# A one-core encoder kernel: order of the MLP's first weight casts, buffers of the pair sums, and place of the last block's left half

## The chip, the cores and the metric

The kernel runs on one core of one Trainium2 chip. The metric is the device time of one execution in microseconds (us), the median of several timed runs. A core has a matrix engine (TensorE, PE in the profile; its weight loads are PEld), a vector engine (VectorE, DVE), an activation engine (ScalarE, ACT), a general engine (GpSimd, POOL) and a queue engine (SyncE, SP) that issues nearly all of the DMA transfers here. Each engine works through its own list of instructions in order and waits at an instruction until its inputs and its output buffer are ready.

## What is computed

One layer of an encoder on two inputs with shared weights: a prompt of 512 rows and a sample of 1024 rows, width 1024. The core of the reference:

```python
def _trunk(x, ...):
    h = _rmsnorm(x, norm_attn_g)
    z = h @ w_in                       # q, k, v and two conv inputs
    a_out = _window_attn(q, k, v, bias, band, attn_sink)
    c = ca * sigmoid(cb)
    c = silu(_layernorm(_dwconv(c, conv_dw_w, conv_dw_b)))   # 31 taps
    x = x + concatenate([a_out, c]) @ w_out
    h = _rmsnorm(x, norm_ffn_g)
    u = _dwconv(h @ w_up, ffn_dw_w, ffn_dw_b)                # 3 taps
    x = x + (silu(u[..., :D_FF]) * u[..., D_FF:]) @ w_down   # D_FF = 2816
    return _rmsnorm(x, norm_final_g)
```

All data are float32. The kernel keeps their precision by splitting each operand into a high part, rounded to the matrix engine's format, and a low part, the rest (`split`, line 227: ACT casts, POOL or DVE subtracts), and by multiplying high by high, high by low and low by high: three matmuls where one would do for rounded numbers.

## The kernel before

**Buffers.** All working tiles come from a host-side list of slots (`Slots`, line 74): 15 of class `q` (4096 bytes in each partition), 4 of class `c` (4224), 61 of class `h` (2048), 2 of class `d` and 32 small ones. A tile takes the smallest free slot that it fits, the one that has been free for longest first, and an argument `among` restricts it to a class. The next user of a slot has to wait for the last reader of the tile that was there.

**Order.** The program is written in one order, and a planner orders each engine's instructions by it and by a simulated time line; an instruction that is written later can be moved ahead when the earlier ones are not ready in that simulation. `tc.issue_after(ins)` binds the instructions written under it to come after `ins` on the engine of `ins`. From line 1381 on the matrix engine's order is the written one (`manual_schedule`); the other engines are still planned. Beside the main stream there is a queue of generators, `side`: after every few matmuls `tick` (line 320) moves it on by as many steps (`yield`) as `pace` says.

**Stages and lines that matter here.**

- Up to about 332 us: the first norm, the combined projection `w_in`, attention and convolution of the prompt. At the end of the prompt's chain, `make_h2` (line 883) scales the prompt's four row blocks, and `transposed` (line 296) turns them on PE in 8 chunks (L301) and evicts each chunk as a high part by ACT (L303) and a low part by DVE (L304). It appends the two eviction instructions of each chunk to the list `marks`, so the last 8 entries are those of the prompt's MLP input. Meanwhile the sample's depthwise convolution of 31 taps goes on: most taps on DVE (L402), five to seven for each piece as a product on ACT (L394) that POOL adds up (L395); DVE adds POOL's sum at the end (L410).
- The prompt's MLP, `for k in range(NJ)` (line 1067), 22 steps from about 332 to 648 us. Each step takes a pair of 1024x128 weight tiles (gate and value half) that were loaded (`want_up_raw`, L224) and split (`want_up`, line 944, by `split`: the cast is L230, the low part L231), and multiplies them with the turned blocks in `up_mm`. The very first half uses the order of L343: for each chunk the high and then the low weights with the high input, and after these the low input with the high weights; all others go by L347, L348 and L350. The first pair is split at lines 1041 and 1042, with no order given. During the MLP, `side` runs `sample` (line 1045): the sample's attention (scores L672), then the loads of `w_out` for its output projection, column half 0 at line 1055 and half 1 at 1064, eight loads there in one go.
- `gate` (line 990) stores each step's result to DRAM (`gt`). For pairs 7 to 10 it calls `pair_sums` (line 1011) directly; for pairs 0 to 6 `pair_sums` runs later from `side` and loads both parts back into a tile of class `c` (L1014). Four POOL steps (L1021 to L1027) write four combinations into a tile `r`, which is stored to DRAM (`gb`, L1028). `r` needs 4096 bytes and so takes a `q` slot, of which the split weights and the loaded ones are also made.
- The sample's output projection by row blocks of 128 (`out_half`, line 828: 24 matmuls for a column half, L838 to L840, then the sum of squares on ACT, L849, and the scale on POOL, L214 and L215), from about 605 to 740 us. `scaled` (line 1101) then multiplies the block by its scale and the norm's weights; for the last four blocks (`t == 1`) it does the right half and the left half (L1110), and forms the sums `s1` (L1085), `s2` and a difference (L1088) with the block's partner, the inputs of a Strassen-like scheme of seven products.
- From about 733 us on, the first products of the sample's up projection run; from about 746 us the last five of seven input combinations are turned in four chunks each (two are turned before) (`turned`, line 1131: transposes L1135, ACT's high part L1137, DVE's low part by `sub`, L1088), between those products (`prod`, L1212 to L1214). These five come in the order 4, 6, 7, 5, 3. Combination 4 needs the right halves alone, 6 needs `s2`. Four PSUM banks take the transposes in turn (`turn_bank`). The products go on to about 1180 us; the down projection follows from about 1165 (L1556 to L1558) and the final norm.

Of the kernel before, what the change touches and what calls it, by code (L numbers as in the profile page):

```python
# [173 lines left out]
def tile_hybrid_encoder(ctx: ExitStack, tc: tile.TileContext, xs, xsT, rel_bias, norm_attn_g, w_in,  # L174
# [16 lines left out]
    sb = Slots(lambda tag: homes[tag[0]], dict(q=(15, 4096), c=(4, 4224), h=(61, 2048), d=(2, 2176), s=(32, 64)), "q", KEEP)  # L191
# [35 lines left out]
    def split(raw, dve=False):  # L227
        shape = list(raw.t.shape[1:])
        hi, lo = sb.tile(shape, F32R), sb.tile(shape, F32R)
        nc.scalar.copy(hi[:], raw[:])  # L230
        ins = (nc.vector if dve else nc.gpsimd).tensor_tensor(lo[:], raw[:], hi[:].bitcast(F32), op=ALU.subtract)  # L231
        if not dve:
            ended["pool"] = ins.ins
        return hi, lo
# [59 lines left out]
    marks = []  # L294
# [39 lines left out]
    def drain(queue):  # L334
        while queue:
            advance(queue)
# [291 lines left out]
    NB = len(blocks)  # L628
# [16 lines left out]
    def sink_columns():  # L645
        for h in range(0, NH, 2):
            t = sb.tile([2, NT])
            for n in range(2):
                nc.vector.tensor_copy(t[:, n, 0:1], nsink[:, h + n:h + n + 1])
            score_rows.append(t)  # L650
# [116 lines left out]
    def attention(u0, u1, then={}):  # L767
        yield from scores(u0)
        for u in range(u0, u1):
            if u + 1 < u1:  # L770
                yield from scores(u + 1)
            yield from values(u)
            if u in then:
                yield from then[u]

    def load_cat(i):
        rawcat[i] = sb.tile([NT])
        nc.sync.dma_start(rawcat[i][:], catd[blocks[i][1]])
# [10 lines left out]
    def conv_norm(i):  # L789
        G, b = blocks[i]  # L790
        if G["g"] == 0:
            drain(convs)
        cat = cat_of(i, 1)
        if i not in cvs:
            load_conv(i)
            yield 0.0
        cv = cvs.pop(i)
        if G["g"] == 1:
            split_cat(i, nc.vector)
        pt = bank("norm")  # L800
        for c in range(4):
            nc.tensor.transpose(pt[:, c * P:(c + 1) * P], cv[:, c, :], ident[:])
        st, mv, rs = sm(6), sm(2), sm(1)
        nc.vector.bn_stats(st[:], pt[:])
        nc.vector.bn_aggr(mv[:], st[:])
        rstd_of(mv[:, 1:2], 1.0, rs[:])
        xh = sb.tile([CCH])
        nc.vector.tensor_scalar(xh[:], pt[:], mv[:, 0:1], rs[:], op0=ALU.subtract, op1=ALU.mult)
        del pt
        for _ in range(YN if G["g"] == 0 else 3):  # L810
            yield 0.0
        p2 = bank("norm")
        for c in range(4):
            nc.tensor.transpose(p2[:, c * P:(c + 1) * P], xh[:, c * P:(c + 1) * P], ident[:])
        y, t = sb.tile([4, P]), sb.tile([4, P])
        for c in range(4):
            nc.scalar.activation(y[:, c, :], p2[:, c * P:(c + 1) * P], AF.Identity,
                                 scale=lng[:, c:c + 1], bias=lnb[:, c:c + 1])
        nc.scalar.activation(t[:], y[:], AF.Tanh)
        nc.vector.scalar_tensor_tensor(t[:], t[:], 1.0, y[:], op0=ALU.add, op1=ALU.mult)  # L820
        nc.scalar.copy(cat[0][:], t[:])
        nc.vector.tensor_tensor(cat[1][:], t[:], cat[0][:].bitcast(F32), op=ALU.subtract)
        yield 0.0
# [33 lines left out]
    def load_wo(kc, n):  # L857
        raw = wor[kc, n] = sb.tile([NT])
        s = slice(n * NT, (n + 1) * NT)
        if kc < 4:  # L860
            for kv in range(NKV):
                r0 = (kv * GRP + kc) * HD
                nc.sync.dma_start(raw[kv * HD:(kv + 1) * HD, :], w_out[0, r0:r0 + HD, s])
        else:
            nc.sync.dma_start(raw[:], w_out[0, kc * P:(kc + 1) * P, s])

    def split_wo(kc, n, dve=False):
        wo[kc, n] = split(wor.pop((kc, n)), dve)
# [52 lines left out]
    def want_up_raw(k, half):  # L921
        if k < len(seq):
            upr[k, half] = chunk_raw(w_up[0], half * FF + seq[k][1] * P)
# [20 lines left out]
    def want_up(k, half):  # L944
        if k < len(seq):
            upw[k, half] = split(upr.pop((k, half)))
# [37 lines left out]
    HT = NT // 2  # L984
# [26 lines left out]
    def pair_sums(p, e=None, o=None):  # L1011
        if e is None:
            g = sb.tile([2, NT], among="c")
            nc.sync.dma_start(g[:], gt[p][:])  # L1014
            yield 0.0
            yield 0.0
            e, o = g[:, 0, :], g[:, 1, :]
        r = sb.tile([4, HT])
        gp = nc.gpsimd.tensor_tensor
        with tc.issue_after(ended["pool"]):  # L1020
            gp(r[:, 0, :], e[:, HR], o[:, HR], op=ALU.add)  # L1021
        yield 0.0
        gp(r[:, 1, :], e[:, HL], e[:, HR], op=ALU.subtract)
        yield 0.0
        gp(r[:, 2, :], r[:, 0, :], e[:, HL], op=ALU.subtract)
        yield 0.0
        gp(r[:, 3, :], o[:, HL], r[:, 2, :], op=ALU.subtract)  # L1027
        nc.sync.dma_start(gb[p][:], r[:])  # L1028
        yield 0.0
# [8 lines left out]
        gate(k, ug[0], uv[0])  # L1038

    use.update(attn="ab", gate="b")  # L1040
    for half in range(2):
        want_up(0, half)
    want_up_raw(1, 0)
    load_bias()
    def sample():
        sink_columns()
        yield from attention(8, 24)
        kt.clear(), vt.clear(), qt.clear(), bias.clear(), score_rows.clear()
        use.update(norm="a")
        pace.update(rate=RN)  # L1050
        for m in range(KC + WOA):
            if m in (2, 4):
                load_cat(m // 2 + 3)
            if m < KC:
                load_wo(m, 0)
            if m >= WOA:
                split_wo(m - WOA, 0, True)
                yield 0.0
        drain(late)
        for m in range(NE):  # L1060
            yield from conv_norm(4 + m)
        load_conv(4 + NE)
        for kc in range(KC):
            load_wo(kc, 1)

    pace.update(rate=RD, late=CD)
    for k in range(NJ):
# [14 lines left out]
    L, R = slice(0, NT), slice(NT, W2)  # L1082

    def add(out, a, b, eng=None):
        (eng or nc.vector).tensor_tensor(out, a, b, op=ALU.add)  # L1085

    def sub(out, a, b, eng=None):
        (eng or nc.vector).tensor_tensor(out, a, b, op=ALU.subtract)  # L1088
# [8 lines left out]
    gFb = sb.tile([D])  # L1097
    nc.sync.dma_start(gFb[:], norm_ffn_g[0].partition_broadcast(P))
    A, rows = {}, {}

    def scaled(i):

        t, b = divmod(i - 4, 4)
        x = rows[t, b] = sb.tile([D])
        if t == 0:
            nc.vector.scalar_tensor_tensor(x[:], x1[i][:], rs2[:, i:i + 1], gFb[:], op0=ALU.mult, op1=ALU.mult)
            x1.pop(i)
            return
        for s in (R, L):
            nc.vector.scalar_tensor_tensor(x[:, s], x1[i][:, s], rs2[:, i:i + 1], gFb[:, s], op0=ALU.mult, op1=ALU.mult)  # L1110
        x1.pop(i)
        e = rows[0, b]
        s1 = rows["s1", b] = sb.tile([NT])
        s2 = rows["s2", b] = sb.tile([NT])
        add(s1[:], x[:, L], x[:, R])
        sub(s2[:], s1[:], e[:, L])
        sub(x[:, L], e[:, L], x[:, L])
        if i >= NB - 2:
            last_sum(b)
# [11 lines left out]
    def turned(i, get):  # L1131
        for c in range(4):
            held, ap = get()
            for b in range(4):
                nc.tensor.transpose(ap[:, b * P:(b + 1) * P], block_rows(i, b)[:, c * P:(c + 1) * P], ident[:])  # L1135
            hi, lo = A[i, c] = (sb.tile([NT], F32R), sb.tile([NT], F32R))
            nc.scalar.copy(hi[:], ap)  # L1137
            sub(lo[:], ap, hi[:].bitcast(F32))
            held = None
            yield 0.0  # L1140
        key = {6: "s2", 5: "s1", 7: 1, 3: 0}.get(i)
        for b in range(4):
            rows.pop((key, b), None)
# [122 lines left out]
    drain(side)  # L1266
    wo.clear()
    cats.clear()
    gFb = None
    for guard in reversed(ps_guards):  # L1270
        guard.__exit__(None, None, None)
    ps2 = [ctx.enter_context(tc.tile_pool(name=f"pw{i}", bufs=1, space=bass.MemoryType.PSUM)) for i in range(2)]
# [25 lines left out]
    def second(j, between=None):  # L1298
        prod(st[j]["x"][:, L], j, 2, False, True, between)
# [88 lines left out]
    def chain(*gens):  # L1388
        for g in gens:
            yield from g  # L1390

    def every(n, gen):

        for c in range(4):
            for _ in range((n * (c + 1)) // 4 - (n * c) // 4):
                next(gen, None)
            yield

    turns = chain(*(turned(i, turn_bank) for i in (4, 6, 7, 5, 3)))
    firsts = []  # L1400
    for j in range(2):
        st[j] = dict(x=wide())
# [4 lines left out]
    second(0, every(7, turns))  # L1407
    fourth(0, every(7, turns), True)
    second(1, chain(every(8, turns)))
    for _ in turns:  # L1410
        raise RuntimeError("turns left")
    pt_guard.__exit__(None, None, None)
# [410 lines left out]
```

## Time and profile before

| what | us |
|---|---|
| median of 3 timed runs | 1498.74 |
| lowest and highest | 1498.42, 1499.70 |
| the profiled execution | 1496.34 |
| its span, first to last instruction | 1494.6 |

The profiled execution is one of its own, with 1.74 us around its span; its granted TensorE clock was 0.996 of the full one on average. In the rows of groups and of the time-ordered view, a line says start, duration, engine, kernel line, operation, tiles (out <- in), shape and count; what stands in brackets is the engine's idle time before, and what ended it. A row of the stretches has the stretch, its length, PE's busy time with the number of matmuls, the granted clock, the DMA engines' share and GB/s. A row of the waits has who waited for whom, the sum, the number and the longest. Successive matmuls overlap: each has a duration of about 0.39 us but the next one starts 0.23 us later.

### The profile page before, as it was taken

Reading aid. Unit: us, or ns where it says so; the run is one execution under the profiler, and the core shown is the slowest. Engines: PE = TensorE matmul, PEld = TensorE weight load, DVE = VectorE, ACT = ScalarE, POOL = GpSimd, SP = SyncE. Lnnn points to the kernel's source line nnn. Section 1 sums busy time; section 2 is a strip of 40 time slices with the busy share of each in tenths; the row PEclk is TensorE's granted clock in tenths of the full one; section 3 lists DMA queues with packets and bytes.
Section 4 is the critical chain, followed back from the end, with each engine's and each line's share of the span. In section 5 each row is a group of like instructions: output and inputs, shape, how many; then the busy total and the mean of one; then the engine's idle time right before and its main releaser. Section 6 shows DMA issues by size and latency. Waiting matters only on the chain.

```text
span 1494.6 us, 19858 instructions
## 1 busy us (share of the span) xinstructions
PE 1474.5 (99%) x6808; PEld 1220.8 (82%) x6808; DVE 1138.6 (76%) x1616; ACT 797.9 (53%) x1417; POOL 682.0 (46%) x540
## 2 busy tenths in 40 slices
PE   9989999999999999999999999999999999999998
PEld 7878888887888888788878888888887888888886
DVE  4999998678689976666768777777776845568884
ACT  7635665335777776543455455544444633434354
POOL 7842444235756566654425555555544000003345
PEclk9999999999999999999999999999999999999999
DMA  8863347275434446783313333333332672356644
GB/s 279 280 199 80 100 120 196 85 221 153 144 112 132 127 133 206 225 287 115 113 57 106 106 106 106 102 99 103 103 109 81 226 264 85 109 173 227 210 173 169
DMA packets 221761, 225.08 MB, mean 151 GB/s; under 512 B 12331, under 2 KB 161843, under 8 KB 221532
## 3 DMA queue, kind: packets, MB, share of 16 engines
q1 hardware_dynamic: 221660, 223.82, 46.7%
q8 instruction: 53, 0.87, 0.2%
q14 instruction: 48, 0.39, 0.1%
HBM read 164.77 MB, written 60.05 MB: 150 GB/s over the span
## 4 chain that ended last, share of the span: by engine, by line
PE 47%; DVE 2%; ACT 1%; issue 0%; DMA 0%; POOL 0%; POOLq 0%; DVEq 0%; ACTq 0%
PE w L1212 9%; PE w L1213 9%; PE w L1214 9%; PE w L1556 7%; PE w L1558 7%; PE w L1557 7%; DVE q L1088 0%; DMA q<-in_w_up 0%; PE t L1135 0%; ACT q L1198 0%; DVE q L1343 0%; DVE q L1342 0%; DVE q L1110 0%; DVE h L1088 0%; ACT h L1137 0%
## 5 line engine op out<-in xcount | busy, mean ns | idle before, releaser
L231 POOL TENSOR_TENSOR q<-q,q 128x1024 fp32r<-128x1024 f32 x71 | 172.7, 2438 | 117.4 <-ACT q L230 42.1
L1088 POOL TENSOR_TENSOR q<-q,q 128x512 fp32r<-128x512 f32 x101 | 142.0, 1413 | 157.4 <-ACT q L1198 145.2
L1088 DVE TENSOR_TENSOR h<-h,h 128x512 fp32r<-128x512 f32 (+2 forms) x202 | 157.3, 811 | 63.0 <-ACT h L1092 26.3
L1558 PE MATMUL w<-h,h 128*128 128x512 f32 x462 | 179.7, 389 | 0.0
L1556 PE MATMUL w<-h,h 128*128 128x512 f32 x458 | 178.2, 389 | 0.0
L1557 PE MATMUL w<-h,h 128*128 128x512 f32 x458 | 178.2, 389 | 0.0
L1212 PE MATMUL w<-h,q 128*128 128x512 f32 x448 | 175.0, 391 | 2.0 <-ACT w L1296 1.4
L1214 PE MATMUL w<-h,q 128*128 128x512 f32 x448 | 174.3, 389 | 0.0
L1213 PE MATMUL w<-h,q 128*128 128x512 f32 x426 | 165.8, 389 | 0.0
L347 PE MATMUL u<-h,q 128*128 128x512 f32 x368 | 146.6, 399 | 0.6 <-ACT q L230 0.6
L348 PE MATMUL u<-h,q 128*128 128x512 f32 x368 | 144.1, 391 | 0.0
L350 PE MATMUL u<-h,q 128*128 128x512 f32 x360 | 141.4, 393 | 0.1
L402 DVE SCALAR_TENSOR_TENSOR c<-c,cvw,c 128x512 f32<-128x512 f32 x184 | 137.8, 749 | 2.6
L1085 POOL TENSOR_TENSOR q<-q,q 128x1024 f32<-128x1024 f32 x12 | 32.5, 2717 | 229.0 <-DMA h<-gb 190.0
L1092 ACT CAST h<-h 128x512 fp32r<-128x512 f32 x120 | 71.9, 620 | 98.2 <-DVE h L1088 41.2
L347 PE MATMUL b<-h,q 128*128 128x512 f32 x264 | 106.1, 402 | 3.9 <-ACT q L230 3.9
L348 PE MATMUL b<-h,q 128*128 128x512 f32 x264 | 104.7, 397 | 0.0
L350 PE MATMUL b<-h,q 128*128 128x512 f32 x264 | 104.3, 396 | 0.0
L1558 PEld LDWEIGHTS w<-h,h 128*128 128x128 f32 x462 | 86.7, 188 | 18.2
L1212 PEld LDWEIGHTS w<-h,q 128*128 128x128 f32 x448 | 84.1, 188 | 20.6 <-ACT w L1296 1.8
L1557 PEld LDWEIGHTS w<-h,h 128*128 128x128 f32 x458 | 86.0, 188 | 17.9
L1556 PEld LDWEIGHTS w<-h,h 128*128 128x128 f32 x458 | 86.0, 188 | 17.7
(447 smaller groups left out, 3641.6 us busy)
## 6 DMA issues: line engine op xcount, KB each, us to landing
q<-in_w_up SPq DMA_DIRECT2D x88, 512.0 KB, 4.1
ga<-q SPq DMA_DIRECT2D x64, 256.0 KB, 2.0
h<-ga SPq DMA_DIRECT2D x57, 256.0 KB, 3.4
q<-in_w_in SPq DMA_DIRECT2D x28, 512.0 KB, 4.9
h<-in_w_down SPq DMA_DIRECT2D x52, 256.0 KB, 3.6
q<-in_x_sample SPq DMA_DIRECT2D x15, 512.0 KB, 7.5
x1d<-q SPq DMA_DIRECT2D x11, 512.0 KB, 2.9
gt<-h SPq DMA_DIRECT2D x22, 256.0 KB, 3.1
```

Source lines behind the costliest of these rows:

```text
L231: ins = (nc.vector if dve else nc.gpsimd).tensor_tensor(lo[:], raw[:], hi[:].bitcast(F32), op=ALU.subtract)
L347: nc.tensor.matmul(out, whi[:, kc, :], hi[:], start=(kc == 0), stop=False)
L348: nc.tensor.matmul(out, whi[:, kc, :], lo[:], start=False, stop=False)
L350: nc.tensor.matmul(out, wlo[:, kc, :], hi[:], start=False, stop=(kc == KC - 1))
L402: nc.vector.scalar_tensor_tensor(acc[:], src(t), w(t), acc[:], op0=ALU.mult, op1=ALU.add)
L1088: (eng or nc.vector).tensor_tensor(out, a, b, op=ALU.subtract)
L1212: nc.tensor.matmul(out, whi[:, s], hi[:], start=(start and c == 0), stop=False, **go)
L1213: nc.tensor.matmul(out, whi[:, s], lo[:], start=False, stop=False, **go)
L1214: nc.tensor.matmul(out, wlo[:, s], hi[:], start=False, stop=(stop and c == 3), **go)
L1556: nc.tensor.matmul(out, sh[:, c], th[:], start=(p == 0), stop=False)
L1557: nc.tensor.matmul(out, sh[:, c], tl[:], start=False, stop=False)
L1558: nc.tensor.matmul(out, sl[:, c], th[:], start=False, stop=(p == NPAIR - 1))
```

## The change

Three groups of edits:

1. The two splits of the MLP's first weight pair are written under `tc.issue_after`: the cast of the first half comes behind ACT's eviction of chunk 2 of the prompt's turned blocks (`marks[-6]`), the cast of the second half behind that of chunk 7 (`marks[-1]`).
2. In `pair_sums` the result tile `r` is taken from class `c` in place of `q`, in the direct calls (pairs 7 to 10) and the later ones (0 to 6). The eight `w_out` loads of column half 1 in `sample` get a `yield` each.
3. For the last row block, `scaled` does the right half alone and keeps the rest for later. `opening` wraps the turning of combination 4: after the second of its four chunks is written it does the left half, `s1`, `s2`, the difference and the last sum (`left_sums`). The tile of the norm's weights, `gFb`, and the block's `x1` are held until then.

```diff
@@ pair_sums
-        r = sb.tile([4, HT])
+        r = sb.tile([4, HT], among="c")
@@ before the prompt's MLP
-    for half in range(2):
-        want_up(0, half)
+    for half, mark in enumerate(marks[-6::5]):
+        with tc.issue_after(mark[0]):
+            want_up(0, half)
@@ sample
         for kc in range(KC):
             load_wo(kc, 1)
+            yield 0.0
@@ scaled
-        for s in (R, L):
+        def part(s):
             nc.vector.scalar_tensor_tensor(x[:, s], x1[i][:, s], rs2[:, i:i + 1], gFb[:, s], op0=ALU.mult, op1=ALU.mult)
+
+        part(R)
+        if i == NB - 1:
+            held.append((i, part))
+        else:
+            left_sums(i, part)
+
+    held = []
+
+    def left_sums(i, part):
+        b = (i - 4) % 4
+        x = rows[1, b]
+        part(L)
         x1.pop(i)
         e = rows[0, b]
         s1 = rows["s1", b] = sb.tile([NT])
...
@@ after the output projection
-    gFb = None
...
@@ the turned combinations
-    turns = chain(*(turned(i, turn_bank) for i in (4, 6, 7, 5, 3)))
+    def opening():
+        for n, _ in enumerate(turned(4, turn_bank)):
+            if n == 1:
+                left_sums(*held.pop())
+            yield
+
+    turns = chain(opening(), *(turned(i, turn_bank) for i in (6, 7, 5, 3)))
...
     second(1, chain(every(8, turns)))
+    gFb = None
```

## The prediction

> **What bounds the kernel now.** I read the page's busy table first, then the busy time in stretches, then the list of what TensorE (PE) waited for, and last the time-ordered view around each wait that the change touches.
>
> ```profile
> span 1494.6 us, 19858 instructions
> PE 1474.5 (99%) x6808; PEld 1220.8 (82%) x6808; DVE 1138.6 (76%) x1616; ACT 797.9 (53%) x1417; POOL 682.0 (46%) x540
> 332.00:342.00 10.00, 7.81 (x46) 1.00 0.94 295
> 740.00:768.00 28.00, 26.13 (x151) 1.00 0.22 69
> 768.00:1120.00 352.00, 351.72 (x1552) 1.00 0.32 103
> ```
>
> PE is busy for 1474.5 of 1494.6 us at a granted clock of 1.00 in these stretches (the column behind the count). In the long stretch from 768 to 1120 us it misses 0.28 us. The number of matmuls doesn't change, so all that the change can win lies in the 20.1 us in which PE is idle: 2.19 of them between 332 and 342, 1.87 between 740 and 768. VectorE (DVE), ScalarE (ACT) and GpSimd (POOL) have spare time; they matter only where PE waits for them:
>
> ```profile
> PE b L347 <- ACT q L230: 3.9, 1, 3.9
> PE a L672 <- DVE h L304: 2.2, 2, 2.0
> PE w L1212 <- ACT w L1296: 1.4, 1, 1.4
> PE t L1135 <- DVE h L1088: 1.3, 1, 1.3
> PE u L347 <- ACT q L230: 0.6, 1, 0.6
> ```
>
> Three of these five belong to the change: L672 behind L304 (the start of the prompt's MLP, where the first weight casts are), the 0.6 at L347 (a weight cast of the later MLP), and L1135 (the turned blocks of the sample). The 3.9 (first projection) and the 1.4 at L1296 (late in the sample's up projection) stand at code that isn't edited. So the ceiling is 2.2 + 0.6 + 1.3 = 4.1 us, and 0.2% of 1498.74, about what a measurement of this kernel tells from no change, is 3.0 us.
>
> **Part 1, the first weight casts.** ACT, DVE, POOL and PE in the stretch of that wait:
>
> ```profile
> 321.67 0.19 ACT L849 ACTIVATION_READ_ACCUMULATOR h<-q 128x1 f32 x1
> 325.35 1.05 ACT L230 CAST q<-q 128x1024 fp32r<-128x1024 f32 x1 [3.49 <-DMA q<-in_w_up]
> 326.31 3.78 ACT L394 ACTIVATE h<-c,cvw 128x512 f32<-128x512 f32 x6
> 330.00 1.82 ACT L303 ACTIVATE h<-a,vecs 128x512 fp32r<-128x512 f32 x3
> 338.42 0.68 ACT L303 ACTIVATE h<-a,vecs 128x512 fp32r<-128x512 f32 x1
> 326.48 2.41 POOL L231 TENSOR_TENSOR q<-q,q 128x1024 fp32r<-128x1024 f32 x1 [3.72 <-PE b L350]
> 330.17 8.11 POOL L395 TENSOR_TENSOR h<-h,h 128x512 f32<-128x512 f32 x6 [1.28 <-ACT h L394]
> 338.31 0.69 DVE L410 TENSOR_TENSOR h<-c,h 128x512 f32<-128x512 f32 x1 [2.23 <-POOL h L395]
> 338.92 1.40 DVE L304 SCALAR_TENSOR_TENSOR h<-a,vecs,h 128x512 fp32r<-128x512 f32 x2
> 328.09 0.49 PE L301 MATMUL a<-ident,q 128*128 128x128 f32 x3
> 332.10 1.07 PE L343 MATMUL u<-h,q 128*128 128x512 f32 x4
> 333.02 0.60 PE L301 MATMUL a<-ident,q 128*128 128x128 f32 x4
> 333.37 0.71 PE L343 MATMUL u<-h,q 128*128 128x512 f32 x2
> 339.71 0.50 PE L672 MATMUL a<-q,h 128*128 128x256 f32 x2 [2.03 <-DVE h L304]
> ```
>
> Read it backwards. PE stood for 2.03 us before L672, for DVE's L304; two of these stood behind L410, which waited for POOL's six conv additions; POOL had begun them only when ACT's six conv products were done (330.17, the products ended at 326.31 + 3.78 = 330.09); and these stood behind the weight cast, which sat on ACT for 3.49 us waiting for its weights to land. The edit puts the cast behind the turned activation of chunk 2, the last of the group of three that ends at 331.82. ACT is then free at 321.86: products to about 325.7, POOL's additions from there to 325.7 + 8.11 = 333.8, or 336.2 when the 2.41 us of the cast's low part goes between them. L410 comes 2.1 us or more earlier than 338.31, and the 2.2 us of idle time go.
>
> What is late next is the weight itself. The turned blocks' last transposes of chunks 0 to 2 end at 328.58, so L303 x3 runs from 328.6 to 330.4, the cast (1.05) to 331.5, and the low part (2.41 on POOL, behind at most one addition of 1.35) ends between 333.9 and 335.3, against 328.89 now. PE wants the high part at 332.10, which holds, and the low part one matmul later, since the first product alternates high and low weights. Twelve transposes (four take 0.35, from 333.02 to the next matmul at 333.37) are other work for 1.05 us; after the first product (0.23) and these, PE would stand from 332.10 + 1.28 = 333.4 to between 333.9 and 335.3: a new wait of 0.5 to 1.9 us, of which I take the smaller half, 0.9. **Part 1: -2.2 + 0.9 = -1.3**, between -2.2 and a loss that I price under the rivals. The second cast, moved behind the last turned activation, costs nothing that PE sees: it can't hold that activation up (338.42 now), and while it and its low part are made, PE has the rest of the 24 products with the first weights, at 0.227 us each (352 / 1552, from the long stretch).
>
> **Part 2, the pair sums' buffers and the spread loads.** Rows around the later cast, and the stores of pair sums:
>
> ```profile
> 607.23 1.05 ACT L230 CAST q<-q 128x1024 fp32r<-128x1024 f32 x1 [3.88 <-DMA gb<-q]
> 608.33 0.50 PE L347 MATMUL u<-h,q 128*128 128x512 f32 x1 [0.59 <-ACT q L230]
> DMA to landing us min/median/max: 2.6/4.2/7.2
> 635.55 0.74 POOL L1021 TENSOR_TENSOR q<-c 128x256 f32<-128x256 f32 x1 [1.72 <-DMA gb<-q]
> ```
>
> The cast's q buffer was a pair sum's result, so the cast waited 3.88 us for that sum's store (the third row: the stores of L1028). With the result in a c buffer the cast can start about 3.8 us sooner and PE's 0.59 us go: **-0.6**. The price is on the four c buffers, which now hold two tiles for each loaded pair: a pair must wait until an earlier store has landed. One such wait is there already (1.72 us, on POOL). More of them, 2.6 to 7.2 us each, fall on POOL, which is idle for half of the span; the work behind them there is the small variance steps for normalised blocks, and one block's output product of 24 matmuls at 0.227, 5.4 us, covers a median store. I count 0, from -0.3 to +1.8 (7.2 less 5.4). The eight `w_out` loads are issued at the same cost on SP, only further apart; what they feed is the output products after the MLP, so 0.
>
> **Part 3, the last block's left half.**
>
> ```profile
> 745.63 0.75 DVE L1110 SCALAR_TENSOR_TENSOR q<-c,rs,q 128x512 f32<-128x512 f32 x1 [1.53 <-POOL rs L215]
> 746.30 1.78 DVE L1110 SCALAR_TENSOR_TENSOR q<-c,rs,q 128x512 f32<-128x512 f32 x1
> 746.24 1.29 POOL L1088 TENSOR_TENSOR q<-h,q 128x512 fp32r<-128x512 f32 x1 [0.65 <-ACT q L1198]
> 748.11 0.69 DVE L1085 TENSOR_TENSOR h<-q 128x512 f32<-128x512 f32 x1
> 748.84 0.69 DVE L1088 TENSOR_TENSOR h<-h,q 128x512 f32<-128x512 f32 x1
> 749.44 0.69 DVE L1088 TENSOR_TENSOR q<-q,q 128x512 f32<-128x512 f32 x1
> 750.05 0.68 DVE L1088 TENSOR_TENSOR h<-t,h 128x512 fp32r<-128x512 f32 x1
> 751.25 4.47 DVE L1088 TENSOR_TENSOR h<-t,h 128x512 fp32r<-128x512 f32 x7
> 746.86 0.59 ACT L1137 CAST h<-t 128x512 fp32r<-128x512 f32 x1 [0.69 <-PE t L1135]
> 747.94 1.07 ACT L1137 CAST h<-t 128x512 fp32r<-128x512 f32 x2 [0.50 <-PE t L1135]
> 749.20 0.27 PE L1135 MATMUL t<-ident,q 128*128 128x128 f32 x1
> 750.78 0.66 PE L1135 MATMUL t<-ident,h 128*128 128x128 f32 x4 [1.31 <-DVE h L1088]
> ```
>
> DVE scales the right half (to 746.38), the left half (to 748.08), forms the sums s1, s2 and the difference (748.11 to 750.13) and only then evicts the low part of the first turned chunk (750.05). PE waits from 749.47 to 750.78 for that eviction, which frees the first of four turn banks, and needs s2 of the last block too. After the edit the left half and its sums are written behind the first two chunks' evictions. DVE has nothing else ready between 746.38 and the end of the first high cast (747.45), so I expect the left half to stay there, then the first eviction (748.08 to 748.7), s1 and s2 by 750.0 with no second eviction between them, or 750.65 with it. The transposes of the next operand start at about 750.1 to 750.7 in place of 750.78. But the third chunk's bank has the same nine DVE steps before it as now (each 0.6), so part of what is won comes back two chunks later. **-0.4**, from -1.3 (all gone) to +0.4: when the left half really goes behind two evictions (the second high cast is done at 748.5, its eviction at 749.2), s2 ends at 749.2 + 0.7 + 0.65 + 0.65 = 751.2, 0.4 later than PE starts now.
>
> The row at 746.30 shows why moving it isn't a free win: 1.78 us where the right half took 0.75, and it ends 0.55 after POOL's step of 746.24 to 747.53. The Trainium skill's page "SBUF — State Buffer", section "Who interferes with whom", says that a VectorE instruction with two SBUF inputs and a GpSimd one that reads SBUF exclude each other, and whoever is first holds the ports to its end. By that rule the 1.03 us are a wait in POOL's shadow, not work that the edit moves; part 3 would be worth nothing and the sum -1.9. The trace agrees with the rule in this pair of rows.
>
> **Sum against the profiled execution:** -1.3 - 0.6 - 0.4 = -2.3 us, a span of 1492.3 for 1494.6. That execution took 1496.34 us, 1.74 around its span, and lies 2.4 below the median of the timed runs; I take the difference off the median: 1498.74 - 2.3 = **1496.4**.
>
> **Rivals.**
> *All three waits close.* For it: each wait has one named cause, and each edit takes that cause away. Against it: part 1 puts the low weights at 333.9 or later. It gives -4.1, 1494.6.
> *The waits only change their place.* PE waits at 333 for low weights instead of at 338 (1.9 of 2.2 back), and the third turned chunk takes back part 3's gain; -0.3 and -0.6 are left, and the planner, which orders the rest anew, puts one wait of the size of its largest (0.6) elsewhere: -0.3, 1498.4. The same number holds if the issue order changes nothing that PE sees.
> *Slower: the low weights queue behind POOL's conv additions.* The engines take their instructions in order, so a place behind all six additions counts in full. If these still start at 330.17 and the low part comes after them, it is ready at 338.28 + 2.41 = 340.7, and PE stands from 333.4: 7.3 us, less the 2.2 that go, +5.1; with parts 2 and 3, +4.1, 1502.8. It decides from the point where the low part is ready later than 333.4 + 2.2 = 335.6, that is, where additions that stand before it end after 333.2. Against it: with ACT free at 321.86 they should start some 4 us sooner, and the weights are wanted first.
>
> **How the numbers follow.** Forecast 0.46, all waits close 0.32, waits only move 0.16, slower 0.06. Faster by over 0.2%: the closing case and 0.04 of the forecast's upper end, 0.36; slower 0.06; within 0.2%, 0.58. The range runs from 1493.8 (the closing case, 0.8 beyond it for the unpriced 1.4 at L1296, should it close by half) to 1499.3 (the moved waits and half of the c buffers' bound): it leaves out the slower case and about as much again.
>
> **What would show it.** Part 1: no idle time before L672, the six products on ACT before the first weight cast, and a short wait of L343 for POOL's L231. Part 2: no weight cast waits for a store to `gb`; more waits of L1021 for such stores. Part 3: the first eviction of a turned chunk before s2, and a wait shorter than 1.31 at the second operand. I am wrong if PE's idle time grows in the planned stretch between 340 and 740 us, where the planner orders everything anew and the largest single wait now is 0.59.

## The result, and the profile after

The changed kernel took **1496.68 us** (median of 20 runs, 1493.09 to 1499.37) against 1498.72 for the kernel before (median of 20 runs, 1495.96 to 1501.79, in turn with it): a ratio of 0.9983 with a 95% interval of 0.9976 to 0.999. That is 2.0 us less; predicted were 2.3 less and 1496.4. The gain is real but under the 0.2% that the prediction set as its bound for "faster". The next sections show that the sum came out right with terms that did not.

The head of the changed kernel's page, and below it what PE waited for (engine, line, whom it waited for: sum, times, longest), its three largest entries (the first also stands in the list of before, with 3.9, at code that isn't edited):

```profile
span 1495.0 us, 19855 instructions
PE 1474.9 (99%) x6808; PEld 1222.4 (82%) x6808; DVE 1142.9 (76%) x1616; ACT 799.9 (54%) x1417; POOL 676.3 (45%) x540
```

```profile
PE b L347 <- ACT q L230: 4.8, 1, 4.8
PE u L347 <- DVE h L967: 2.5, 2, 1.5
PE u L839 <- DVE h L231: 2.0, 1, 2.0
```

The three waits that the change aimed at, L672 behind L304, L347 behind the later cast L230 and L1135 behind L1088, are all gone. In their place stand two new ones: L347 behind L967 (an eviction of the MLP) and L839 behind L231 (the low part of a weight of the output projection). The span, 1495.0, is even 0.4 longer than the span shown of before. So that one profile of before needs a second look. The same kernel, profiled again (e1 below), has this head and these waits:

```profile
span 1499.4 us, 19858 instructions
PE 1476.8 (98%) x6808; PEld 1221.6 (81%) x6808; DVE 1142.6 (76%) x1616; ACT 797.7 (53%) x1417; POOL 680.1 (45%) x540
```

```profile
PE a L672 <- DVE h L304: 2.6, 2, 2.5
PE u L347 <- ACT q L230: 2.3, 1, 2.3
...
PE t L1135 <- DVE h L1088: 1.3, 1, 1.3
```

The same three waits as before, but the middle one is 2.3 in place of 0.6, and the span 4.8 longer. The profile on which the prediction was made was a short execution of the kernel before (1496.34 us, with medians of 1498.5 to 1499.8), and that of e1 is a long one (1501.2 us); the runs in turn, not the spans, say what the change is worth.

The views by stretch (stretch, its length, PE's busy time with the number of matmuls, granted clock, DMA share, GB/s) place the difference. The kernel before, its second profile, and the changed kernel:

```profile
330.00:400.00 70.00, 67.81 (x327) 1.00 0.53 168
550.00:670.00 120.00, 119.03 (x568) 1.00 0.74 238
745.00:800.00 55.00, 53.24 (x270) 1.00 0.23 69
```

```profile
330.00:400.00 70.00, 67.38 (x317) 0.98 0.53 166
550.00:670.00 120.00, 116.30 (x549) 1.00 0.73 233
745.00:800.00 55.00, 53.17 (x270) 1.00 0.21 63
```

```profile
330.00:400.00 70.00, 68.30 (x327) 1.00 0.48 151
550.00:670.00 120.00, 117.06 (x552) 0.99 0.75 240
745.00:800.00 55.00, 54.88 (x281) 1.00 0.24 72
```

PE's idle time is the length less the busy time. In the last stretch it falls from 1.76 and 1.83 to 0.12: this gain is in every profile of the changed kernel. In the first stretch the changed kernel misses 1.70, less than both profiles of before (2.19 and 2.62); in the second its 2.94 lies between the two (0.97 and 3.70). What happened there can't be read from one profile of each, hence the experiments.

### The profile page after: what moved, and what is told of

Same layout as the page of the kernel before. It is cut to its first block, busy times and chain, and to the rows that moved or that the text cites. A ratio compares the mean times of both kernels' runs of the same rounds, so it can differ in the third digit from the quotient of the medians.

```text
span 1495.0 us, 19855 instructions
## 1 busy us (share of the span) xinstructions
PE 1474.9 (99%) x6808; PEld 1222.4 (82%) x6808; DVE 1142.9 (76%) x1616; ACT 799.9 (54%) x1417; POOL 676.3 (45%) x540
## 4 chain that ended last, share of the span: by engine, by line
PE 51%; DMA 3%; DVE 2%; POOL 2%; issue 1%; ACT 1%; SPq 0%; POOLq 0%; DVEq 0%; ACTq 0%
PE w L1227 9%; PE w L1228 9%; PE w L1229 9%; PE w L1578 7%; PE w L1577 7%; PE w L1579 7%; DMA c<-gt 2%; DMA gb<-c 1%; PE u L838 1%; PE u L840 1%; PE u L839 1%; DVE h L231 1%; DVE q L1090 0%; PE c L838 0%; PE c L839 0%
## 5 line engine op out<-in xcount | busy, mean ns | idle before, releaser
L231 POOL TENSOR_TENSOR q<-q,q 128x1024 fp32r<-128x1024 f32 x71 | 172.0, 2429 | 95.9 <-ACT q L230 28.2
L347 PE MATMUL u<-h,q 128*128 128x512 f32 x368 | 146.7, 399 | 2.5 <-DVE h L967 2.5
L350 PE MATMUL u<-h,q 128*128 128x512 f32 x360 | 141.4, 393 | 0.3
L347 PE MATMUL b<-h,q 128*128 128x512 f32 x264 | 105.6, 400 | 4.8 <-ACT q L230 4.8
L350 PE MATMUL b<-h,q 128*128 128x512 f32 x264 | 103.9, 395 | 0.0
```

Of the source, the lines that this page charges most:

```text
L347: nc.tensor.matmul(out, whi[:, kc, :], hi[:], start=(kc == 0), stop=False)
L350: nc.tensor.matmul(out, wlo[:, kc, :], hi[:], start=False, stop=(kc == KC - 1))
```

## The experiments

Kernels e1 to e4, e5 to e8, and e9 to e11 were each timed in one session on one chip, in turn with the kernel before, and e12 in a session of its own. The median of before was 1498.48, 1499.41, 1499.13 and 1499.77 us in these four, so kernels of different sessions are compared by the ratio, which is taken over the runs in turn and isn't exactly that of the medians. "Idle" is worked out as above from the same view by stretch of each kernel (330 to 400, 550 to 670, 745 to 800 us); the last column is span less PE busy, from the page.

| kernel | median us | ratio to before, 95% interval | idle 330-400 | 550-670 | 745-800 | whole span |
|---|---|---|---|---|---|---|
| e1 before, again | 1500.28 | 1.0004 (0.9992 to 1.0016) | 2.62 | 3.70 | 1.83 | 22.6 |
| e2 changed, again | 1496.46 | 0.9984 (0.9971 to 0.9996) | 1.19 | 2.55 | 0.14 | 20.2 |
| e3 part 1 alone | 1499.20 | 1.0001 (0.9989 to 1.0013) | 2.11 | 2.75 | 1.75 | 22.4 |
| e11 part 2 alone | 1496.77 | 0.9982 (0.9971 to 0.9993) | 2.06 | 2.77 | 0.10 | 20.1 |
| e4 part 3 alone | 1498.68 | 0.9993 (0.9982 to 1.0005) | 3.24 | 2.42 | 0.69 | 20.1 |
| e6 part 2, buffers only | 1501.93 | 1.0018 (1.0007 to 1.0029) | 2.58 | 6.88 | 1.30 | 25.8 |
| e7 part 2, loads only | 1499.12 | 0.9999 (0.9988 to 1.0010) | 2.09 | 1.70 | 1.59 | 20.2 |
| e5 `gFb` held only | 1498.56 | 0.9995 (0.9983 to 1.0007) | 3.17 | 2.74 | 0.74 | 22.2 |
| e8 changed + casts behind eviction | 1493.49 | 0.9963 (0.9948 to 0.9977) | 0.17 | 2.57 | 0.32 | 18.6 |
| e12 the same as e8 | 1493.66 | 0.9958 (0.9944 to 0.9971) | 0.15 | 2.47 | 0.30 | 18.4 |
| e9 e8, direct sums only in `c` | 1498.62 | 0.9995 (0.9985 to 1.0005) | 0.19 | 3.69 | 1.42 | 19.5 |
| e10 e8 without part 2 | 1495.98 | 0.9981 (0.9970 to 0.9992) | 0.28 | 1.47 | 0.58 | 16.8 |

### Both kernels again, and parts 1 and 3 alone (e1 to e4)

No edit in e1 and e2. e3 has only part 1, e4 only part 3:

```diff
@@ e3
-    for half in range(2):
-        want_up(0, half)
+    for half, mark in enumerate(marks[-6::5]):
+        with tc.issue_after(mark[0]):
+            want_up(0, half)
@@ e4
+        part(R)
+        if i == NB - 1:
+            held.append((i, part))
+        else:
+            left_sums(i, part)
...
-    gFb = None
...
+    turns = chain(opening(), *(turned(i, turn_bank) for i in (6, 7, 5, 3)))
...
+    gFb = None
```

> The kernel before, unchanged, profiled a second time. The first profile of the changed kernel is no shorter than the first one of the kernel before (1495.0 against 1494.6 us of span) although the medians of 20 runs differ by 2.0 us. Theory A (the profiled execution of before was a lucky one): the waits of PE before L672 (2.0 us), at L1135 (1.3 us) and at L347 behind ACT's cast (0.6 us) stand here again at the same places, within 0.5 us each, and the span is 1 to 4 us longer than 1494.6. Theory B (the waits that the change removed belong to one execution, not to the program's order): at least one of the three is missing or under half of its size.

> The changed kernel, profiled a second time. Its first profile shows three waits of PE that the kernel before does not have: 1.55 us before L347 (bank held by L967) at 347 us, 0.9 us before L347 at 618 us and 2.0 us before L839 behind DVE's L231 at 656 us. Theory A (they come from the changed order): all three stand here again, within 0.5 us each. Theory B (they come from transfers that were late in that one execution): at least one of them is missing or under half of its size, and the span after 332 us is shorter by that.

> Only the order of the first weight casts. Theory A (the prediction's part 1): no idle time before L672, a wait of at most 1 us for the low part of the first weights, 1.3 us less than before. Theory B (the wait moves on: PE comes earlier to the next weights, whose loads land at the same time, so ACT's cast for them holds up ACT's eviction L971 and PE waits for the bank at 347 us): the wait of about 1.5 us before L347 stands in this kernel too, and the gain is 0.3 to 0.7 us. The waits at 607 us (0.6) and 749 us (1.3) stay in both.

> Only the last block's left half moved. Theory A (the prediction's part 3): the first eviction of a turned chunk comes before s2 and the difference, the wait of 1.3 us at L1135 is 0.4 us shorter or more. Theory B (this edit leaves VectorE's order as it was and the wait went in the changed kernel for another reason, for instance because the block before it was ready earlier relative to PE): the wait of about 1.3 us at L1135 stays, gain 0 to 0.2 us.

e2 repeats the result (0.9984). **Part 1 alone shows no gain** (1.0001, that is -1.6 to +1.9 us), though its wait at L672 is gone. The time-ordered view of the changed kernel shows why (start, duration, engine, line, operation, tiles; in brackets the idle time before and what ended it):

```profile
322.79 4.15 ACT L394 ACTIVATE h<-c,cvw 128x512 f32<-128x512 f32 x6 [1.19 <-PE b L350]
328.14 1.85 ACT L303 ACTIVATE h<-a,vecs 128x512 fp32r<-128x512 f32 x3 [1.21 <-PE a L301]
329.87 1.05 ACT L230 CAST q<-q 128x1024 fp32r<-128x1024 f32 x1
...
327.01 4.04 POOL L395 TENSOR_TENSOR h<-h,h 128x512 f32<-128x512 f32 x3 [4.50 <-ACT h L394]
331.01 2.38 POOL L231 TENSOR_TENSOR q<-q,q 128x1024 fp32r<-128x1024 f32 x1
333.35 4.03 POOL L395 TENSOR_TENSOR h<-h,h 128x512 f32<-128x512 f32 x3
...
343.14 1.05 ACT L230 CAST q<-q 128x1024 fp32r<-128x1024 f32 x1 [4.02 <-DMA q<-in_w_up]
...
345.50 0.78 ACT L971 ACTIVATE h<-u,vecs,fw 128x512 f32<-128x512 f32 x1
...
346.31 0.75 DVE L967 SCALAR_TENSOR_TENSOR h<-u,fw,h 128x511 f32<-128x511 f32 x1 [3.43 <-ACT h L971]
...
348.52 0.47 PE L347 MATMUL u<-h,q 128*128 128x512 f32 x1 [1.55 <-DVE h L967]
```

The first six rows are the prediction's step: the products first on ACT, then the activations, then the cast; the low part ends at 331.01 + 2.38 = 333.39, and PE doesn't wait for it. The next rows are what the prediction didn't look at. ACT's following instructions are the casts of step 1's weights. The first of them waits 4.02 us for its weights to land. Behind it, in ACT's order, stand a second one and then the eviction L971 of the first product, which starts at 345.50, though the last matmul of that product ended at 341.27 (in the next section's rows L971 starts at 341.10). L971 and L967 free the PSUM bank, so PE waits 1.55 us for it at 348.52 (1.03 in e2, 1.96 in e3). In e3 this is about what went at L672: its idle time from 330 to 400 us is 2.11, against 2.19 and 2.62 before. This is the same pattern as the wait that was removed: a cast that waits for a landing weight, with work that PE needs queued behind it on ACT.

### The casts of step 1 behind the eviction (e8, e12)

If that is the cause, binding those casts behind the first L971 must take the new wait away, and nothing else is needed. The edit, on the changed kernel:

```diff
@@ up_half (first eviction)
-            nc.scalar.activation(u[:], pu[n][:], AF.Identity, scale=w(1), bias=...)
+            ended["evac"] = nc.scalar.activation(u[:], pu[n][:], AF.Identity, scale=w(1), bias=...).ins
@@ ffn_step
-        want_up(k + 1, 0)
+        with (tc.issue_after(ended["evac"]) if k == 0 else nullcontext()):
+            want_up(k + 1, 0)
+        first_evac = ended["evac"]
...
-        want_up(k + 1, 1)
+        with (tc.issue_after(first_evac) if k == 0 else nullcontext()):
+            want_up(k + 1, 1)
```

> The changed kernel, and in addition the two casts of the second step's weights bound behind ACT's eviction of the first product (L971). Theory A (PE's wait of 1.0 to 2.0 us at 347 us comes from that eviction standing on ACT behind casts that wait for weights to land): the wait at 347 us goes and nothing of more than 0.5 us takes its place before 370 us; 1.0 to 1.5 us less than the changed kernel. Theory B (PE is by then limited by the landing of the weights themselves): PE waits as long for L347 or L350 behind ACT's cast or POOL's low part, no gain.

> The version with the next casts behind the eviction, timed and profiled a second time, since its first timing (0.9963, six runs) is 2.0 parts in a thousand below the changed kernel's (0.9983), more than the 1.0 to 1.5 us that the wait at 347 us is worth. Theory A (the gain is that wait): ratio to before 0.9970 to 0.9980, no wait over 0.5 us between 342 and 370 us, the waits at 616 (0.4), 654 (2.1) and 688 us (0.9) stand again. Theory B (the whole stretch got better): ratio 0.9965 or less and one of these three waits is gone.

In e8's time-ordered view the eviction now stands ahead of the casts, and in the stretch PE misses 0.17 us:

```profile
341.10 0.78 ACT L971 ACTIVATE h<-u,vecs,fw 128x512 f32<-128x512 f32 x1 [2.17 <-PE u L343]
342.36 1.06 ACT L230 CAST q<-q 128x1024 fp32r<-128x1024 f32 x1 [0.48 <-DMA q<-in_w_up]
```

```profile
330.00:400.00 70.00, 69.83 (x339) 1.00 0.48 149
```

L971 starts at 341.10 instead of 345.50, and the cast is no later for it. That the blocked cast caused the wait is thereby shown. This kernel is the best of the study: 0.9963 (0.9948 to 0.9977) and 0.9958 (0.9944 to 0.9971), 5 to 6 us under before and about 3 us under the changed kernel. Its idle time over the whole span is 18.6 and 18.4 against 20.1 and 20.2, so some 1.6 of these 3 us are located as idle time. The rest isn't another wait: PE's other waits of the MLP and the output projection still stand in e8 and e12 (at L839 2.1 and 1.8, at L814 0.9 and 0.7, at L347 behind a later L967 0.4 and 0.7). The last section shows a candidate, the clock after a wait.

### Part 2 and its halves (e11, e6, e7)

e11 has both edits of part 2, e6 only the first, e7 only the second:

```diff
@@ pair_sums (e6, e11)
-        r = sb.tile([4, HT])
+        r = sb.tile([4, HT], among="c")
@@ sample (e7, e11)
         for kc in range(KC):
             load_wo(kc, 1)
+            yield 0.0
```

> Only the pair sums' results in c buffers. Theory A (the price of four c buffers that each hold a loaded pair or a result): the wait of ACT's cast at 607 us (0.6 to 2.8 us of PE in four profiles) is gone, and a wait of about 2 us of PE for a w_out part (L839 behind VectorE's L231) stands at about 656 us, because POOL's sums wait for loads into c buffers: gain 0 to 1 us. Theory B (that wait comes from the spread loads): no wait over 0.5 us at 656, gain 0.6 to 2.8 us.

> Only the eight w_out loads spread by a step each. Theory A (no cost and no gain of its own): the wait at 607 us stays (0.6 to 2.8), no wait over 0.5 us at 656 us, time within 0.7 us of before. Theory B (loads that are written later land later, and PE waits for w_out parts): a wait of about 2 us at L839 or L838 between 645 and 665 us.

> Both edits of part 2 and nothing else. Theory A (the spread of the loads takes back what the c buffers cost, 5.4 us at 657 us when alone): the wait at L839 is 1 to 3 us, the cast's wait at 607 is gone, time within 1 us of before. Theory B (the spread does nothing for it, and the smaller wait in the changed kernel is due to parts 1 or 3): a wait of 4 us or more at L839, 2 to 3 us slower than before.

The buffers alone make the kernel slower (1.0018, interval above 1), the spread loads alone do nothing (0.9999), and **both together give as much as the whole change** (0.9982, e11, against 0.9984, e2), more than the 1 us that was expected of e11. The price of the buffers is the longest wait in e6's list, 5.4 us at L839 behind L231, and the time-ordered view of e6 leads to its cause:

```profile
656.24 0.74 POOL L1021 TENSOR_TENSOR c<-c 128x256 f32<-128x256 f32 x1 [7.01 <-DMA c<-gt]
...
658.31 1.26 POOL L998 TENSOR_TENSOR h<-h,h 128x512 f32<-128x512 f32 x1
...
659.61 0.62 ACT L230 CAST h<-h 128x512 fp32r<-128x512 f32 x1 [10.95 <-POOL h L998]
...
660.26 1.23 DVE L231 TENSOR_TENSOR h<-h,h 128x512 fp32r<-128x512 f32 x1 [7.13 <-ACT h L230]
...
663.12 0.79 PE L839 MATMUL u<-h,h 128*128 128x512 f32 x1 [5.44 <-DVE h L231]
```

Read from the top: POOL stands 7.01 us for a pair's load. A loaded pair now takes two of the four `c` buffers, so by the program no more than two pairs are in flight, and a load may have to wait for a store (SyncE's list of waits in e6 has one that does, for 1.1 us). The load in question was issued at 649.64, right behind the store of the pair before at 649.26, and POOL could go on 6.6 us later. Behind that step POOL has the MLP's last gate product, L998; the cast of a `w_out` weight needs the `h` buffer that L998 frees and has waited 10.95 us on ACT; DVE's low part needs the cast, and PE the low part: 5.44 us. In the changed kernel, with the loads spread, the same chain is there but shorter:

```profile
651.26 1.29 POOL L998 TENSOR_TENSOR h<-h,h 128x512 f32<-128x512 f32 x1 [4.00 <-DVE h L967]
653.68 0.84 POOL L1021 TENSOR_TENSOR c<-c 128x256 f32<-128x256 f32 x1 [1.13 <-DMA c<-gt]
...
657.71 1.20 DVE L231 TENSOR_TENSOR h<-h,h 128x512 fp32r<-128x512 f32 x1 [3.70 <-POOL c L1025]
...
658.96 0.79 PE L839 MATMUL u<-h,h 128*128 128x512 f32 x1 [2.00 <-DVE h L231]
```

Here L998 comes ahead of the pair's steps, and what DVE waits for is a direct pair's sum that still reads the buffer which the low part is to fill. PE waits 2.00 instead of 5.44 (2.1 in e2, 1.7 in e11). Over all profiles, the stretch that part 2 was meant for does not shrink. From 550 to 670 us the five without part 2 (before, e1, e3, e4, e5) miss 0.97 to 3.70 us, 2.5 on average, and the five with the whole of it (changed, e2, e11, e8, e12) 2.5 to 2.9, 2.7 on average: the wait at the later cast goes and others of the same size come. What the profiles show of part 2's gain is in 745 to 800, where e11 misses 1.7 us less than both profiles of before. The rest of its 2.7 us (-4.3 to -1.0) isn't located.

That 1.7 was forecast for part 3, not for part 2. With part 2 alone the wait at L1135 vanishes as well, and e11's rows show how:

```profile
746.18 1.42 DVE L1111 SCALAR_TENSOR_TENSOR q<-c,rs,q 128x512 f32<-128x512 f32 x2 [1.53 <-POOL rs L215]
...
749.01 1.78 POOL L1089 TENSOR_TENSOR q<-h,q 128x512 fp32r<-128x512 f32 x1 [2.86 <-ACT q L1199]
```

The two halves of the last block take 1.42 together; POOL's step, which began at 746.24 beside the left half before, now comes behind them. (The lines are one further down than before.) Its input, a cast on ACT, was made at 748.31 instead of 745.53. Why the cast moved is not shown; the next section tests one way to move it.

### Which part of part 3 works (e5)

e4 removes 1.1 of the 1.83 us of idle time in the last stretch; the wait at L1135 falls from 1.31 to 0.28. But DVE's order is the old one. These rows are e4's:

```profile
748.58 1.42 DVE L1110 SCALAR_TENSOR_TENSOR q<-c,rs,q 128x512 f32<-128x512 f32 x2 [1.53 <-POOL rs L215]
...
750.76 0.69 DVE L1088 TENSOR_TENSOR h<-h,q 128x512 f32<-128x512 f32 x1
...
751.97 0.68 DVE L1088 TENSOR_TENSOR h<-t,h 128x512 fp32r<-128x512 f32 x1
...
754.80 1.29 POOL L1088 TENSOR_TENSOR q<-h,q 128x512 fp32r<-128x512 f32 x1 [6.25 <-ACT q L1211]
...
752.71 0.66 PE L1148 MATMUL t<-ident,h 128*128 128x128 f32 x4 [0.28 <-DVE h L1088]
```

Right half, left half, sums and only then the first eviction (the row at 751.97), as before the change. What differs is that both halves take 1.42 together, where before the left one alone took 1.78, and that POOL's L1088, then at 746.24 beside the left half, now comes at 754.80. So there are two explanations: the place where the left half is written, or the tile `gFb` that is held longer, so that the weight part which POOL works on gets another buffer, later. e5 is the kernel before with the second alone:

```diff
-    gFb = None
...
     second(1, chain(every(8, turns)))
+    gFb = None
```

> The kernel before with one line moved: the tile of the norm's weights (gFb) is kept until the turned combinations are done, and the last block's left half stays where it was. Theory A (buffers: keeping that tile makes the cast of a weight part take another q buffer, so ACT's cast and POOL's low part come some 8 us later and VectorE's scaling of the left half no longer meets POOL's step): the left half takes about 0.75 us and not 1.78, and the wait at L1135 falls from 1.3 to about 0.3 us, as with the whole edit. Theory B (moving the left half is what counts): the left half still takes 1.78 us and the wait of 1.3 us stays.

```profile
750.11 1.41 DVE L1110 SCALAR_TENSOR_TENSOR q<-c,rs,q 128x512 f32<-128x512 f32 x2 [1.53 <-POOL rs L215]
...
756.33 1.29 POOL L1088 TENSOR_TENSOR q<-h,q 128x512 fp32r<-128x512 f32 x1 [6.25 <-ACT q L1198]
...
754.24 0.66 PE L1135 MATMUL t<-ident,h 128*128 128x128 f32 x4 [0.29 <-DVE h L1088]
```

The same picture and the same wait of 0.29 without moving the left half at all. The 1.31 - 0.28 = 1.03 us that PE gains are the 1.78 - 0.75 = 1.03 that the left half had lost beside POOL. The time of the whole kernel (0.9993 in e4, 0.9995 in e5, both intervals reach over 1) is too coarse to show 1 us; the rows show it. In e11 the same step of POOL is out of the way for another reason, with the same effect.

### Is the price of the buffers worth paying? (e9, e10)

Two attempts to better e8: e9 gives only the direct sums a `c` buffer, since only the loaded pairs hold two of the four; e10 takes part 2 out altogether.

```diff
@@ e9
-        r = sb.tile([4, HT], among="c")
+        r = sb.tile([4, HT], among="c" if p >= SOON else "q")
@@ e10
-        r = sb.tile([4, HT], among="c")
+        r = sb.tile([4, HT])
...
-            yield 0.0
```

> The version with the next casts behind the eviction, and c buffers for the direct pair sums alone; the sums of loaded pairs take q buffers again. Theory A (the 2.0 to 5.4 us at 656 us come from POOL standing on a loaded pair's load into a c buffer, with the MLP's gate product and the direct sums queued behind it): the wait at L839 goes or falls under 0.7 us, the wait of ACT's cast at 607 us stays away, 1 to 3 us less than that version (1493.5). Theory B (the wait comes from w_out parts that are late in any case): it stays at about 2 us, no gain.

> The version with the next casts behind the eviction, but with the whole of part 2 undone (pair sums in q buffers, loads not spread). Theory A (part 2 pays, as predicted, 0.6 us): PE's idle time between 550 and 745 us grows by 0.5 us or more over the 3.5 us of that version, with the cast behind a store at 607 us back. Theory B (part 2 costs more than it gives): it falls to 1 to 3.7 us, the range of the four profiles with q buffers, and the time is 0 to 1.5 us below that version's.

e9's list of waits:

```profile
PE u L838 <- ACT h L230: 2.1, 1, 2.1
...
PE a L814 <- DVE h L808: 1.2, 1, 1.2
PE w L1230 <- ACT h L1428: 1.0, 1, 1.0
PE u L839 <- DVE h L231: 0.5, 1, 0.5
```

The wait at L839 fell from 2.1 (e8) to 0.5, but two others came, 2.1 at L838 and 1.0 at L1230, and the one at L814 grew from 0.9 to 1.2; the kernel is back at 0.9995. That is some 5 us over e8, of which the profiles locate 0.9 as idle time. e10 has the least idle time of all profiles, 16.8 us, and yet it is slower than e8: 0.9981 against 0.9963 and 0.9958, some 3 us. Its profiled execution, 1493.58 us, was the fastest of its 12 runs (up to 1499.0), so the profile is not one of its median. Where the 3 us are isn't shown, and so it isn't shown either what part 2 is worth on top of e8; with results in `q` buffers the later cast waits for a store's landing again (1.1 here, 0.6 and 2.3 in the two profiles of before, 2.8 in e3), a wait that differs from run to run.

## Why the prediction was right

The total, -2.3 predicted and -2.0 measured, was right; by terms it was wrong in three places that nearly cancelled, so that it came out is in good part luck. In the table, the rows of the parts are ratios of kernels that have one part alone, times 1498.7.

| step | predicted | measured alone |
|---|---|---|
| part 1 | -2.2 + 0.9 = -1.3 | +0.1 (-1.6 to +1.9) |
| part 2 | -0.6 | -2.7 (-4.3 to -1.0) |
| part 3 | -0.4 | -1.0 (-2.7 to +0.7) |
| sum | -2.3 | -3.6; all three in one kernel -2.4 (-4.3 to -0.6) in e2 |

**Part 1.** The mechanism and the times of its own steps held: products first, additions from 327.01, the low part ready at 333.39 where 333.9 to 335.3 was predicted, no idle time at L672. The new wait of 0.9 for the low weights did not come: eight transposes stood ahead of it at 331.85, and PE's only wait for a low part of these weights there is 0.16 to 0.17 at L350, for the second cast, in e2, e3, e8 and others. The step that failed is "a new wait of 0.5 to 1.9 us, of which I take the smaller half" as the only price: PE came earlier to a bank whose eviction stood behind casts blocked on landing weights, 1.0 to 2.0 us at L967. The prediction's rows ended at the stretch of the wait it removed; the instructions next in ACT's order were not read. That the second cast "costs nothing that PE sees" is right to those 0.17 us.

**Part 2.** The cast came off the store as forecast, and its wait was mis-sized: 0.6 in the profile at hand, 2.3 in the second one. But the step "PE's 0.59 us go" as a gain failed, since other waits took its place in that stretch (2.5 us idle without part 2, 2.7 with it). The price counted at 0 failed: "one block's output product of 24 matmuls at 0.227, 5.4 us, covers a median store" looks at the output product that the pair sums feed, whereas L998 and the `h` buffer of a weight cast are what stands behind a blocked POOL: 5.4 us for the buffers alone, which is beyond the bound of +1.8 too. And the 0 for the spread loads failed in the other sense: they do nothing alone, but with the buffers they bring the 5.4 down to about 2.

**Part 3.** "The left half to stay there, then the first eviction" with s1 and s2 behind it failed: the order on DVE didn't change, and the eviction still comes behind the sums. The prediction weighed the Trainium skill's page "SBUF — State Buffer", section "Who interferes with whom" (a VectorE instruction with two SBUF inputs and a GpSimd one that reads SBUF exclude each other), and concluded that by it part 3 would be worth nothing. The runs agree with the rule, 1.78 beside POOL and half of 1.42 without; the conclusion from it was the error, since the edit, by holding a buffer, moved POOL's instruction away. On top of part 2 it adds nothing that can be seen: e11 without it has 0.10 us of idle time in the stretch, the changed kernel 0.12. So the sum of the parts counts this wait twice; it can be most of the 1.2 us between the last row's two numbers, each of which is uncertain by 1.7 us or more.

**Rivals.** "The waits only change their place" described the mechanism of part 1 well, with the place wrong. The slower case, low weights behind six additions, did not occur: POOL put the low part after three of them. The prediction said that it would be wrong if PE's idle time grew between 340 and 740 us. It did grow there, to 4.91 (400 us less 395.09 busy; 4.38 in e2), from 1.13 in the first profile of before (398.87) and from 3.86 in the second (396.14), so by its own sign the account of this stretch was wrong:

```profile
340.00:740.00 400.00, 398.87 (x1918) 1.00 0.49 159
```

```profile
340.00:740.00 400.00, 396.14 (x1894) 1.00 0.49 157
```

```profile
340.00:740.00 400.00, 395.09 (x1893) 1.00 0.49 157
```

The total was saved by the part of the wait at L672 that lies ahead of 340 and by 745 to 800.

**The ceiling.** That "all that the change can win lies in the 20.1 us in which PE is idle" failed too. After some waits the clock is halved for a while, which the next section shows, so a wait can cost more than its length.

## What to carry to other kernels

When a wait goes, read the next instructions of every engine in it up to the next buffer that PE needs: an engine that works in order and stands at a transfer holds back all evictions behind it, and binding such a cast behind the eviction cost nothing here and gave more than the whole change. A new use of a scarce buffer is priced by what is queued behind the engine that will wait for it, not by the consumer of the data. Before an edit's effect is put down to where code was moved, look whether it moved a buffer: holding one tile longer did all that moving the left half did. And one profile is one execution: two of the same kernel differed here by 4.8 us in their spans, more than twice what was forecast.

## What the runs showed of the hardware

**The spread and the clock.** The same program spread by 3 to 4 us to either side of its median, and the time goes with the run's mean granted clock: of 102 runs of the kernel before, the 4 at 0.994 have a median of 1503.3 us, the 13 at 0.995 1500.9, the 31 at 0.996 1500.1, the 41 at 0.997 1498.6 and the 13 at 0.998 1497.5.

**A short wait can be paid for twice.** These are the 3.4 us behind the wait at L672, in the kernel before and in its second profile, where that wait was 2.0 and 2.5 us:

```profile
341.40:344.80 3.40, 3.40 (x17) 1.00 0.89 253
```

```profile
341.40:344.80 3.40, 3.40 (x10) 0.51 1.03 274
```

At about half the clock, PE did 10 matmuls instead of 17; the same ten matmuls of L343, from 341.18 and 341.05 on, took 2.43 us in the one and 4.03 in the other, 1.6 us more, none of it idle time. Behind 300 us the 14 profiles have 16 waits of PE of 1.9 us or more. Ten of them, of 1.9 to 5.4 us, are followed by such a stretch: the one at L672 in e1, e4, e5 and e11, those at L967 and at the later cast in e3, the 2.0 at L839 in the changed kernel, the 5.4 in e6 (there it begins within the wait), one of 2.2 at 746 in e7 and one of 2.1 in e9. Six are not, of 1.9 to 2.4 us. No such stretch stands behind 300 us without such a wait. The Trainium skill's page "TensorE: Matmul & The Clock Gate", section "Part 1: The HAM clock gate", has the clock fall after an idle window of about 3.4 us; here it fell after nine waits shorter than that, but not after every one of their length.

This bears on e8. Its edit takes the last wait out of the stretch from 330 to 400 us, and its runs have a mean clock of 0.9977, those of e12 0.9974, against 0.9966 in the 20 runs of the changed kernel, 0.9962 in e2 and 0.9965 in the 102 of before. A difference of 0.001 is 1.5 us, so the clock can make up the part of e8's gain that isn't idle time. In e6, slower than before by some 2.7 us, it is 0.9949; in e9 and e10, slower than e8, 0.9963 and 0.9965. These are means that go together; no run changes the clock alone.
